# A decoder block on one core: the last 512 columns of the embedding gate, one token half after the other

## The chip, the cores and the metric

The kernel runs on one core of a Trainium2 chip. The metric is the device time of one execution in microseconds (us). TensorE (PE) does the matmuls, VectorE (DVE) and ScalarE (ACT) the elementwise work, GpSimd (POOL) a few small operations, and SyncE (SP) issues most transfers.

## The reference

One pre-norm decoder layer over 256 tokens and 2048 channels. Only the last step matters here:

```
x    = x + merged @ w_o                            # (256, 2048)
e    = rms_norm(p @ w_ple, g_ple_post)             # (256, 2048)
gate = sigmoid(rms_norm(x, g_ple) @ w_ple_gate)    # w_ple_gate is 2048 x 2048
x    = x + gate * e
out  = rms_norm(x, g_final)                        # over the 2048 channels of a token
```

The last norm needs the sum of squares over all 2048 channels of a token before any channel of that token can be written out. Inputs and outputs are fp32.

## The kernel before

Tokens are held in two halves of 128 (`h` is 0 or 1), one token per partition. Every large matrix product is made of three products, to keep fp32 precision: each weight and each activation is split into a high part (a copy in a reduced format, `fp32r`) and a low part (the rest), and high x high, high x low and low x high are added up in PSUM.

Weights stream in as *units*, `[128, 1024]` pieces of 512 KB. `issue_unit` issues the load of unit s + 7 on SyncE's queue into one of five `raw` buffers, `unit_hi` (L249, ScalarE) makes the high part of unit s + 3, `unit_lo` (L261, VectorE) the low part of unit s + 2; `hi` and `lo` have four buffers each. The loop over the units (`for s in range(NU)`) emits for each unit its matmuls, then these preparations, then what earlier units deferred. Tile's planner then sets the order on each engine by its own estimate of times and by what is ready; the order of the code is a priority and not the order of execution. A tile taken by `slot(tag, ...)` has one buffer for each tag, so a new tile waits until the last reader of the old one is done.

The embedding gate is four blocks of 512 output columns (`NC` = 4, `CW` = 512), each of eight units in `block_tm`. A unit holds 2 x 128 of the 2048 input channels (`kt`) for 512 columns. Here the activations `x2h` and `x2l` are the stationary operand (128 x 128) and the weights the moving one (128 x 512), so a unit has 12 matmuls, six for each token half, and the two halves fill two PSUM tiles side by side:

```
for h in range(2):
    for k in range(2):
        mm(ps, ah[:, kt, hs], hi[:, w], start=kt == 0, stop=False)
        mm(ps, ah[:, kt, hs], lo[:, w], start=False, stop=False)
        mm(ps, al[:, kt, hs], hi[:, w], start=False, stop=kt == kts - 1)
```

When a block is complete, `ev_pg` evacuates it for each half: the sigmoid with the token's scale (L638, ScalarE), times `e` (L641, VectorE), added to `x2` (L642), squared with the sum kept in `sq3` (L643, ScalarE), and times the gain of the last norm (L644, VectorE). `main_ps` has three PSUM tiles.

After the loop, once for both halves: `rstd_tok` reduces the sums (L625), scales them (L626) and takes the power -0.5 on GpSimd (L628); then `x2` is scaled in four pieces of 128 x 1024, one of each half on ScalarE (L1144) and one on VectorE (L1146), and each piece is written by a transfer of 512 KB on SyncE's queue (L1147). The tags `S2` and `S3` held `mh` and `ml`, the activations of the product with `w_o`, which is complete before the gate's blocks begin.

Of the kernel before, what the change touches and what calls it, by code (L numbers as in the profile page):

```python
# [10 lines left out]
F32R = mybir.dt.float32r  # L11
I32 = mybir.dt.int32
AF = mybir.ActivationFunctionType
ALU = mybir.AluOpType
AX = mybir.AxisListType
# [3 lines left out]
P = 128  # L19
T = 256  # L20
D = 2048
KT = 16
EPS = 1e-6
# [6 lines left out]
NC = 4  # L30
CW = 512
NWARM = 30
BUDGET = 1.3
TRLAG = 2

C_U, C_ZS, C_CQ, C_K, C_V, C_ZA, C_KI, C_GS, C_GA = 0, 1024, 2048, 2560, 2816, 3072, 4096, 4176, 6224

# [5 lines left out]
def block_kernel(ctx: ExitStack, tc: tile.TileContext, A: dict, out: bass.AP):  # L43
    nc = tc.nc
    V, S, G, PE = nc.vector, nc.scalar, nc.gpsimd, nc.tensor
    TT, STT = nc.vector.tensor_tensor, nc.vector.scalar_tensor_tensor

    cp = ctx.enter_context(tc.tile_pool(name="cp", bufs=1))
    wp = ctx.enter_context(tc.tile_pool(name="wp", bufs=4))
    ev = ctx.enter_context(tc.tile_pool(name="ev", bufs=2))  # L50
# [7 lines left out]
    def nm(s):  # L58
        uid[0] += 1
        return f"{s}_{uid[0]}"  # L60

    def slot(tag, shape, dt=F32):
        return cp.tile(shape, dt, tag=tag, name=nm(tag))

    def const(s, shape, dt=F32):
        return cp.tile(shape, dt, tag=s, name=s)
# [4 lines left out]
    def main_ps():  # L71
        return pm.tile([P, 512], F32, tag="main", name=nm("main"))
# [60 lines left out]
    mhalf = const("mhalf", [P, 2])  # L133
# [4 lines left out]
    def mm(o, l, r, start=True, stop=True, **kw):  # L138
        PE.matmul(o, l, r, start=start, stop=stop, **kw)  # L139
# [44 lines left out]
    units = []  # L184
    deferred = []
    step = [0]

    def defer(n, fn):
        deferred.append((step[0] + n, fn))

    def run_deferred(flush=False):
        while True:
            due = [d for d in deferred if flush or d[0] <= step[0]]
            if not due:
                return
            for d in due:
                deferred.remove(d)
            for d in due:
                d[1]()
# [36 lines left out]
            advance(t)  # L236

    his, los = {}, {}

    def unit_hi(u):  # L240
        if u >= len(units):
            return
        cols = units[u][2]
        hi = wp.tile([P, 1024], F32R, tag="hi", name=nm("hi"))
        src = raws[u][:, :cols]
        q = 2 if u < 3 else 1
        for i in range(q):
            o = slice(i * cols // q, (i + 1) * cols // q)
            S.copy(hi[:, o], src[:, o])  # L249
        his[u] = hi  # L250

    def unit_lo(u):
        if u >= len(units):
            return
        cols = units[u][2]
        lo = wp.tile([P, 1024], F32R, tag="lo", name=nm("lo"))
        src = raws.pop(u)
        q = 2 if u < 3 else 1
        for i in range(q):
            o = slice(i * cols // q, (i + 1) * cols // q)  # L260
            TT(lo[:, o], src[:, o], his[u][:, o].bitcast(F32), ALU.subtract)  # L261
        los[u] = lo
# [11 lines left out]
    def flush():  # L274
        run_deferred(True)
# [26 lines left out]
    def block_tm(act, kts, evac, needs=None):  # L302

        st = {}
        n = kts // 2

        def go(i, hi, lo):
            ah, al = act()
            if i == 0:
                st["ps"] = [main_ps(), None]  # L310
            for h in range(2):
                if st["ps"][h] is None:
                    st["ps"][h] = main_ps()
                ps = st["ps"][h]
                hs = slice(h * P, (h + 1) * P)
                for k in range(2):
                    kt = 2 * i + k
                    w = slice(k * CW, (k + 1) * CW)
# [3 lines that stand above are left out]
                if i == n - 1:  # L322
                    defer(h, lambda h=h, ps=ps: evac(h, ps))
        return [(lambda hi, lo, i=i: go(i, hi, lo), (needs or {}).get(i)) for i in range(n)]

    def add_tm(us):
        if len(us) == 1:
            us = us + [None]
        for a, b in zip(us[::2], us[1::2]):
            add_chunk(a, b)  # L330
# [10 lines left out]
        return (go, need)  # L341


    R = {}

    def hilo(ap):
        return ap[:, 0], ap[:, 1]
# [37 lines left out]
    u = slot("S5", [P, 8, T])  # L385
# [20 lines left out]
    for nb in range(8):  # L406
        add_chunk(*block_k16(xact, ev_u(nb), acc=first_acc(nb) if nb < 2 else None,
                             late=(6, 5, 3, 2)[nb] if nb < 4 else 1, split=nb < 2))
# [135 lines left out]
    def ccol(nb):  # L544
        return slice(nb * CW, (nb + 1) * CW)
# [11 lines left out]
    def tmp():  # L557
        R["ri"] += 1
        return R["ring"][:, R["ri"] % 4, :]
# [18 lines left out]
    def ev_ao(nb):  # L578
# [5 lines left out]
        def f(h, ps):  # L584
# [9 lines left out]
            if h == 1:  # L594
                defer(TRLAG, lambda: to_channels(R["os"], nb, tr))
        return f

    def ev_o(nb):
# [9 lines left out]
        def f(h, ps):  # L608
# [8 lines left out]
            if h == 1:  # L617
                defer(TRLAG, lambda: to_channels(R["x2"], nb, tr))
                if nb == NC - 1:
# [3 lines left out]
    def rstd_tok(sq, denom, tag):  # L623
        v = const(tag + "_v", [P, 2])
        V.tensor_reduce(v, sq, AX.X, ALU.add)  # L625
        V.tensor_scalar(v, v, 1.0 / denom, EPS, ALU.mult, ALU.add)  # L626
        c = const(tag + "_c", [P, 2])
        G.tensor_tensor(c, v, mhalf, ALU.pow)  # L628
        return c

    def ev_pg(nb):
        def f(h, ps):
            if nb == 0 and h == 0:
                R["sq3"] = const("sq3", [P, 2, NC])
            c = ccol(nb)
            x2 = R["x2"][:, h, c]
            s = tmp()
            S.activation(s, ps, AF.Sigmoid, scale=R["r2"][:, h:h + 1])  # L638

            def g():  # L640
                TT(s, s, R["e"][:, h, c], ALU.mult)  # L641
                TT(x2, x2, s, ALU.add)  # L642
                S.activation(s, x2, AF.Square, accum_out=R["sq3"][:, h, nb:nb + 1])  # L643
                TT(x2, x2, R["gfin"][:, c], ALU.mult)  # L644
            defer(0 if nb == NC - 1 else 1, g)
        return f


    sm = {}
# [444 lines left out]
        add_chunk(es[0][0], es[1][0])  # L1094
    for nb in range(NC):
        add_tm(block_tm(lambda: (R["mh"], R["ml"]), KT, ev_o(nb), {4: [pre_gate(A["xtok"], nb)]}))
    for nb in range(NC):
        add_tm(block_tm(lambda: (R["x2h"], R["x2l"]), KT, ev_pg(nb), {7: ["et"]} if nb == 0 else None))
    assert sum(1 for c in chunks if c[0] == "w") == NCH, (len(chunks), NCH)


# [18 lines left out]
    for s in range(NU):  # L1120
# [11 lines left out]
        unit_lo(s + 2)  # L1132
        issue_unit()
        pump(BUDGET)
    while deferred:
        step[0] += 1
        run_deferred()

    r3 = rstd_tok(R["sq3"], D, "r3")
    for h in range(2):  # L1140
        for q in range(2):
            o = R["x2"][:, h, q * 1024:(q + 1) * 1024]
            if q == 0:
                S.activation(o, o, AF.Copy, scale=r3[:, h:h + 1])  # L1144
            else:
                V.tensor_scalar(o, o, r3[:, h:h + 1], None, ALU.mult)  # L1146
            nc.sync.dma_start(out[h, :, q * 1024:(q + 1) * 1024], o)  # L1147


def _prepare(i):  # L1150
# [101 lines left out]
```

## Time and profile before

| what | value |
|---|---|
| runs shown, us | 809.04, 809.75, 854.57 (median 809.75) |
| profiled execution, us | 808.27 |
| its span, us | 806.5 |
| mean granted TensorE clock | 0.989 |
| TensorE busy | 783.9 us, 97% |
| VectorE, ScalarE busy | 575.3 us, 396.9 us |

The span goes from the first to the last instruction of the profiled execution; its own time is 1.77 us longer. A busy share is an average over the whole span. Start times in the rows below are us from the start of the span, and a granted clock of 1.00 is 2.4 GHz, 0.50 is 1.2 GHz.

### The profile page before, as it was taken

Reading aid. Unit: us, or ns where it says so; the run is one execution under the profiler, and the core shown is the slowest. Engines: PE = TensorE matmul, PEld = TensorE weight load, DVE = VectorE, ACT = ScalarE, POOL = GpSimd, SP = SyncE. Lnnn points to the kernel's source line nnn. Section 1 sums busy time; section 2 is a strip of 40 time slices with the busy share of each in tenths; the row PEclk is TensorE's granted clock in tenths of the full one; section 3 lists DMA queues with packets and bytes.
Section 4 is the critical chain, followed back from the end, with each engine's and each line's share of the span. In section 5 each row is a group of like instructions: output and inputs, shape, how many; then the busy total and the mean of one; then the engine's idle time right before and its main releaser. Section 6 shows DMA issues by size and latency. Waiting matters only on the chain.

```text
span 806.5 us, 12813 instructions
## 1 busy us (share of the span) xinstructions
PE 783.9 (97%) x5032; PEld 675.8 (84%) x5032; DVE 575.3 (71%) x891; ACT 396.9 (49%) x539; POOL 8.4 (1%) x17
## 2 busy tenths in 40 slices
PE   8999999999998999999999999999999999999993
PEld 7999987777997888899999987887887888888882
DVE  6999854999999954454668877756688555556662
ACT  7544545543444744453455474544445444445542
POOL 0000000000000000000000000000000000000000
PEclk9999999999999999999999999999999999999997
DMA  8868765346663676634754656666766665555522
GB/s 316 282 215 228 226 202 173 126 157 209 212 206 98 206 245 212 216 111 143 240 190 147 201 160 230 226 226 224 254 205 234 215 207 186 182 183 183 184 78 104
DMA packets 52060, 158.06 MB, mean 196 GB/s; under 512 B 5920, under 2 KB 12064, under 8 KB 51616
## 3 DMA queue, kind: packets, MB, share of 16 engines
q1 hardware_dynamic: 47104, 150.67, 56.6%
q10 hardware_dynamic: 4896, 6.58, 2.3%
q8 instruction: 39, 0.64, 0.3%
q14 instruction: 21, 0.17, 0.1%
HBM read 147.79 MB, written 8.39 MB: 194 GB/s over the span
## 4 chain that ended last, share of the span: by engine, by line
PE 38%; issue 11%; ACT 1%; DVE 0%; ACTq 0%; POOLq 0%; POOL 0%
PE main L139 34%; PE aux L139 2%; PE aux L147 1%; DVE lo L261 0%; ACT hi L249 0%; DVE S L1033 0%; ACT S L1144 0%; ACTq L1247 0%; ACT S L581 0%; POOLq L1247 0%; POOL r_c L628 0%; ACT S L1034 0%; PE small L147 0%; DVE r_v L626 0%; DVE r_v L625 0%
## 5 line engine op out<-in xcount | busy, mean ns | idle before, releaser
L261 DVE TENSOR_TENSOR lo<-raw,hi 128x1024 fp32r<-128x1024 f32 (+2 forms) x259 | 309.7, 1198 | 170.0 <-ACT hi L249 169.7
L249 ACT CAST hi<-raw 128x1024 fp32r<-128x1024 f32 (+2 forms) x259 | 265.4, 1031 | 319.7 <-PE main L139 282.7
L139 PE MATMUL main<-hi,S 128*128 128x512 f32 x544 | 175.2, 397 | 0.9 <-ACT S L1034 0.9
L139 PE MATMUL main<-lo,XH 128*128 128x512 f32 (+1 forms) x416 | 162.2, 390 | 1.9 <-DVE lo L261 1.9
L139 PE MATMUL main<-hi,XH 128*128 128x512 f32 (+1 forms) x416 | 163.4, 393 | 0.0
L139 PE MATMUL main<-hi,XL 128*128 128x512 f32 (+1 forms) x416 | 161.8, 389 | 0.0
L139 PE MATMUL main<-XH,hi 128*128 128x256 f32 x448 | 127.5, 285 | 1.8 <-ACT hi L249 1.8
L139 PE MATMUL main<-XH,lo 128*128 128x256 f32 x448 | 126.7, 283 | 1.9 <-DVE lo L261 1.9
L139 PE MATMUL main<-XL,hi 128*128 128x256 f32 x448 | 126.4, 282 | 0.0
L139 PEld LDWEIGHTS main<-hi,S 128*128 128x128 f32 x544 | 102.2, 188 | 25.3 <-ACT S L1034 1.6
L139 PE MATMUL main<-lo,S 128*128 128x512 f32 x272 | 107.8, 396 | 0.0
L139 PEld LDWEIGHTS main<-lo,XH 128*128 128x128 f32 x416 | 78.0, 188 | 20.4 <-DVE lo L261 3.5
L139 PEld LDWEIGHTS main<-hi,XH 128*128 128x128 f32 x416 | 78.0, 187 | 18.3
L139 PEld LDWEIGHTS main<-hi,XL 128*128 128x128 f32 x416 | 78.0, 187 | 17.4
L139 PEld LDWEIGHTS main<-XH,hi 128*128 128x128 f32 x448 | 85.1, 190 | 2.3 <-ACT hi L249 2.1
L139 PEld LDWEIGHTS main<-XH,lo 128*128 128x128 f32 x448 | 85.1, 190 | 2.1 <-DVE lo L261 2.1
L139 PEld LDWEIGHTS main<-XL,hi 128*128 128x128 f32 x448 | 85.1, 190 | 0.1
L139 PE MATMUL main<-S,hi 128*128 128x256 f32 x384 | 69.3, 283 | 0.1
L139 PEld LDWEIGHTS main<-lo,S 128*128 128x128 f32 x272 | 51.2, 188 | 11.0
L139 PEld LDWEIGHTS main<-S,hi 128*128 128x128 f32 x384 | 58.9, 188 | 1.7 <-issue 1.0
L139 PE MATMUL main<-S,lo 128*128 128x256 f32 x192 | 53.8, 280 | 0.0
L139 PEld LDWEIGHTS main<-S,lo 128*128 128x128 f32 x192 | 36.1, 188 | 0.0
(205 smaller groups left out, 616.5 us busy)
## 6 DMA issues: line engine op xcount, KB each, us to landing
raw<-in_wts_dram SPq DMA_DIRECT2D x247, 512.0 KB, 3.9
raw<-in_wvk_dram SPq DMA_DIRECT2D x8, 336.0 KB, 2.9
gs_d<-big ACTq DMA_DIRECT2D x8, 256.0 KB, 3.6
ga_d<-big ACTq DMA_DIRECT2D x8, 256.0 KB, 4.4
big<-gs_d SPq DMA_DIRECT2D x8, 256.0 KB, 4.6
big<-ga_d SPq DMA_DIRECT2D x8, 256.0 KB, 3.7
S<-in_grow_dram SPq DMA_DIRECT2D x2, 1024.0 KB, 6.0
big<-in_xtok_dram SPq DMA_DIRECT2D x8, 256.0 KB, 3.7
```

What stands on the lines that cost most here:

```text
L139: PE.matmul(o, l, r, start=start, stop=stop, **kw)
L147: PE.matmul(o, i, idn, is_transpose=True)
L249: S.copy(hi[:, o], src[:, o])
L261: TT(lo[:, o], src[:, o], his[u][:, o].bitcast(F32), ALU.subtract)
```

## The change

The first three blocks of the gate stay as they are. In the last block, the eight units in the loop serve the first token half alone (`last_half0`), with all 512 columns, six matmuls a unit; their high and low parts are kept. For this, four of the eight units take their parts from the tags `S2` and `S3` instead of the four turning buffers (`unit_tile`). After the loop the second token half is done in two parts of 256 columns, each over all eight units (96 matmuls with 256 columns instead of 48 with 512). Between the two parts `finish_half(0)` is written: sum of squares, power, scaling and output of the first half. The parts of the second half are evacuated one by one (`pg_part`), with a column of `sq3` for each, and `finish_half(1)` ends the kernel. The output is scaled and written in eight pieces of 128 x 512 (256 KB): those of the first half all on SyncE's queue, those of the second half alternately on ScalarE's and SyncE's.

```diff
--- before.py
+++ after.py
@@ -32,6 +32,7 @@
 NWARM = 30
 BUDGET = 1.3
 TRLAG = 2
+LASTU = 8
 
 C_U, C_ZS, C_CQ, C_K, C_V, C_ZA, C_KI, C_GS, C_GA = 0, 1024, 2048, 2560, 2816, 3072, 4096, 4176, 6224
 
@@ -236,12 +237,22 @@
             advance(t)
 
     his, los = {}, {}
+    R = {}
+
+    def unit_tile(tag, u):
+
+        j = u - (len(units) - LASTU)
+        if 0 <= j < LASTU - 4:
+            if j == 0:
+                R[tag + "x"] = slot("S2" if tag == "hi" else "S3", [P, LASTU - 4, 1024], F32R)
+            return R[tag + "x"][:, j, :]
+        return wp.tile([P, 1024], F32R, tag=tag, name=nm(tag))
 
     def unit_hi(u):
         if u >= len(units):
             return
         cols = units[u][2]
-        hi = wp.tile([P, 1024], F32R, tag="hi", name=nm("hi"))
+        hi = unit_tile("hi", u)
         src = raws[u][:, :cols]
         q = 2 if u < 3 else 1
         for i in range(q):
@@ -253,7 +264,7 @@
         if u >= len(units):
             return
         cols = units[u][2]
-        lo = wp.tile([P, 1024], F32R, tag="lo", name=nm("lo"))
+        lo = unit_tile("lo", u)
         src = raws.pop(u)
         q = 2 if u < 3 else 1
         for i in range(q):
@@ -341,7 +352,6 @@
         return (go, need)
 
 
-    R = {}
 
     def hilo(ap):
         return ap[:, 0], ap[:, 1]
@@ -628,22 +638,66 @@
         G.tensor_tensor(c, v, mhalf, ALU.pow)
         return c
 
+    def pg_part(ps, h, c, j, late=0):
+        x2 = R["x2"][:, h, c]
+        n = c.stop - c.start
+        s = tmp()[:, :n]
+        S.activation(s, ps[:, :n], AF.Sigmoid, scale=R["r2"][:, h:h + 1])
+
+        def g():
+            TT(s, s, R["e"][:, h, c], ALU.mult)
+            TT(x2, x2, s, ALU.add)
+            S.activation(s, x2, AF.Square, accum_out=R["sq3"][:, h, j:j + 1])
+            TT(x2, x2, R["gfin"][:, c], ALU.mult)
+        defer(late, g)
+
     def ev_pg(nb):
         def f(h, ps):
             if nb == 0 and h == 0:
-                R["sq3"] = const("sq3", [P, 2, NC])
-            c = ccol(nb)
-            x2 = R["x2"][:, h, c]
-            s = tmp()
-            S.activation(s, ps, AF.Sigmoid, scale=R["r2"][:, h:h + 1])
-
-            def g():
-                TT(s, s, R["e"][:, h, c], ALU.mult)
-                TT(x2, x2, s, ALU.add)
-                S.activation(s, x2, AF.Square, accum_out=R["sq3"][:, h, nb:nb + 1])
-                TT(x2, x2, R["gfin"][:, c], ALU.mult)
-            defer(0 if nb == NC - 1 else 1, g)
+                R["sq3"] = const("sq3", [P, 2, NC + 1])
+                V.memset(R["sq3"], 0.0)
+            pg_part(ps, h, ccol(nb), nb, 0 if nb == NC - 1 else 1)
         return f
+
+    last = []
+
+    def last_half0():
+
+        ev = ev_pg(NC - 1)
+
+        def go(i, hi, lo):
+            last.append((hi, lo))
+            if i == 0:
+                R["ps0"] = main_ps()
+            last_mm(R["ps0"], 0, i, slice(0, CW))
+            if i == LASTU - 1:
+                defer(0, lambda: ev(0, R["ps0"]))
+        return [(lambda hi, lo, i=i: go(i, hi, lo), None) for i in range(LASTU)]
+
+    def last_mm(ps, h, i, c):
+        hi, lo = last[i]
+        ah, al = R["x2h"], R["x2l"]
+        n = c.stop - c.start
+        hs = slice(h * P, (h + 1) * P)
+        for k in range(2):
+            kt = 2 * i + k
+            w = slice(k * CW + c.start, k * CW + c.stop)
+            mm(ps[:, :n], ah[:, kt, hs], hi[:, w], start=kt == 0, stop=False)
+            mm(ps[:, :n], ah[:, kt, hs], lo[:, w], start=False, stop=False)
+            mm(ps[:, :n], al[:, kt, hs], hi[:, w], start=False, stop=kt == KT - 1)
+
+    def finish_half(h):
+        v = const(f"r3v{h}", [P, 2])
+        V.tensor_reduce(v[:, 0:1], R["sq3"][:, h], AX.X, ALU.add)
+        V.tensor_scalar(v[:, 0:1], v[:, 0:1], 1.0 / D, EPS, ALU.mult, ALU.add)
+        G.tensor_tensor(v[:, 1:2], v[:, 0:1], mhalf[:, 0:1], ALU.pow)
+        for q in range(4):
+            o = R["x2"][:, h, ccol(q)]
+            if q % 2 == 0:
+                S.activation(o, o, AF.Copy, scale=v[:, 1:2])
+            else:
+                V.tensor_scalar(o, o, v[:, 1:2], None, ALU.mult)
+            (nc.scalar if h and q % 2 == 0 else nc.sync).dma_start(out[h, :, ccol(q)], o)
 
 
     sm = {}
@@ -1094,8 +1148,9 @@
         add_chunk(es[0][0], es[1][0])
     for nb in range(NC):
         add_tm(block_tm(lambda: (R["mh"], R["ml"]), KT, ev_o(nb), {4: [pre_gate(A["xtok"], nb)]}))
-    for nb in range(NC):
+    for nb in range(NC - 1):
         add_tm(block_tm(lambda: (R["x2h"], R["x2l"]), KT, ev_pg(nb), {7: ["et"]} if nb == 0 else None))
+    add_tm(last_half0())
     assert sum(1 for c in chunks if c[0] == "w") == NCH, (len(chunks), NCH)
 
 
@@ -1132,19 +1187,20 @@
         unit_lo(s + 2)
         issue_unit()
         pump(BUDGET)
-    while deferred:
-        step[0] += 1
-        run_deferred()
-
-    r3 = rstd_tok(R["sq3"], D, "r3")
-    for h in range(2):
-        for q in range(2):
-            o = R["x2"][:, h, q * 1024:(q + 1) * 1024]
-            if q == 0:
-                S.activation(o, o, AF.Copy, scale=r3[:, h:h + 1])
-            else:
-                V.tensor_scalar(o, o, r3[:, h:h + 1], None, ALU.mult)
-            nc.sync.dma_start(out[h, :, q * 1024:(q + 1) * 1024], o)
+    flush()
+    parts = [slice(0, CW // 2), slice(CW // 2, CW)]
+    pss = []
+    for j, c in enumerate(parts):
+        pss.append(main_ps())
+        for i in range(LASTU):
+            last_mm(pss[j], 1, i, c)
+        if j == 0:
+            finish_half(0)
+    base = (NC - 1) * CW
+    for j, c in enumerate(parts):
+        pg_part(pss[j], 1, slice(base + c.start, base + c.stop), NC - 1 + j)
+        flush()
+    finish_half(1)
 
 
 def _prepare(i):
```

## Rows read from the trace of the kernel before

**Rows 1.** The page's first part: busy us of each engine (share of the span).

```profile
PE 783.9 (97%) x5032; PEld 675.8 (84%) x5032; DVE 575.3 (71%) x891; ACT 396.9 (49%) x539; POOL 8.4 (1%) x17
```

**Rows 2.** Windows: us, PE, PEld, DVE, ACT, POOL busy, PEclk, DMA share, GB/s.

```profile
770.95:773.75 2.80, 2.80 (x13) 2.25 (x13) 2.52 (x4) 2.25 (x4) 0.00 (x0) 1.00 0.58 190
```

**Rows 3.** Timeline of the tail: start us, us, engine, line, operation [idle].

```profile
792.96 0.39 PE L139 MATMUL main<-hi,XL 128*128 128x512 f32 x1
...
793.38 0.69 ACT L638 ACTIVATE S<-main,r_c 128x512 f32<-128x512 f32 x1 [0.71 <-PE main L139]
...
794.83 0.69 DVE L642 TENSOR_TENSOR S<-S,S 128x512 f32<-128x512 f32 x1
...
795.55 0.63 ACT L643 ACTIVATE S<-S 128x512 f32<-128x512 f32 x1 [0.67 <-DVE S L642]
...
796.92 0.15 DVE L625 TENSOR_REDUCE r_v<-sq 128x2 f32<-128x8 f32 x1
...
797.36 0.69 POOL L628 TENSOR_TENSOR r_c<-r_v,mhalf 128x2 f32<-128x2 f32 x1 [90.98 <-DVE r_v L626]
...
798.08 1.42 DVE L1146 TENSOR_SCALAR S<-S,r_c 128x1024 f32<-128x1024 f32 x2 [0.80 <-POOL r_c L628]
798.86 2.94 SPq L1147 DMA_DIRECT2D out_dram<-S  x4
```

**Rows 4.** Short windows of the output and of an earlier load, columns as above.

```profile
799.50:800.00 0.50, 0.00 (x0) 0.00 (x0) 0.00 (x0) 0.50 (x1) 0.00 (x0) 0.50 0.63 254
...
802.00:802.50 0.50, 0.00 (x0) 0.00 (x0) 0.00 (x0) 0.00 (x0) 0.00 (x0) 0.50 1.04 410
...
804.50:805.00 0.50, 0.00 (x0) 0.00 (x0) 0.00 (x0) 0.00 (x0) 0.00 (x0) 0.50 0.73 279
...
555.20:556.00 0.80, 0.80 (x6) 0.62 (x5) 0.66 (x3) 0.45 (x2) 0.00 (x0) 1.00 0.79 264
```

**Rows 5.** Timeline of TensorE, starts of matmuls of 512 and of 256 columns.

```profile
354.74 0.28 PE L139 MATMUL main<-XL,hi 128*128 128x256 f32 x1
...
361.37 0.28 PE L139 MATMUL main<-XH,hi 128*128 128x256 f32 x1
...
779.89 0.39 PE L139 MATMUL main<-hi,XH 128*128 128x512 f32 x1
```

**Rows 6.** Timeline of SyncE, VectorE and ScalarE ahead of the last units.

```profile
745.32 25.53 SPq L97 DMA_DIRECT2D raw<-in_wts_dram  x10
...
772.07 1.22 DVE L261 TENSOR_TENSOR lo<-raw,hi 128x1024 fp32r<-128x1024 f32 x1 [0.24 <-ACT hi L249]
...
773.81 0.68 DVE L644 TENSOR_TENSOR S<-S,S 128x512 f32<-128x512 f32 x1
...
782.23 1.05 ACT L249 CAST hi<-raw 128x1024 fp32r<-128x1024 f32 x1 [1.75 <-PE main L139]
...
783.31 1.23 DVE L261 TENSOR_TENSOR lo<-raw,hi 128x1024 fp32r<-128x1024 f32 x1 [1.57 <-ACT hi L249]
```

**Rows 7.** DMA issues: tensors, queue, count, KB each, median us to landing.

```profile
raw<-in_wts_dram SPq DMA_DIRECT2D x247, 512.0 KB, 3.9
...
S<-in_pT_dram SPq DMA_DIRECT2D x1, 256.0 KB, 2.7
```

**Rows 8.** Groups by line and form, 256 columns: busy us, mean ns of one.

```profile
L418 ACT ACTIVATE big<-t 128x256 f32<-128x256 f32 x16 | 6.7, 420 | 34.0 <-DVE t L416 34.0
...
L416 DVE TENSOR_TENSOR t<-main,row 128x256 f32<-128x256 f32 x16 | 6.6, 414 | 0.6 <-PE main L139 0.6
...
L982 DVE TENSOR_SCALAR S<-S,sums 128x256 f32<-128x256 f32 x8 | 2.4, 347 | 0.0
```

**Rows 9.** One line's instructions: transfer issues on ScalarE, ns min/median/max.

```profile
L426 ACTq DMA_DIRECT2D gs_d<-big x8: 326/326/327, 133.9 to 211.9; - x8
```

**Rows 10.** Windows early in the kernel, columns as in rows 2.

```profile
7.00:10.00 3.00, 2.26 (x6) 1.12 (x6) 2.85 (x7) 3.00 (x8) 0.00 (x0) 1.00 1.00 386
...
12.00:14.00 2.00, 2.00 (x12) 2.00 (x11) 0.62 (x2) 2.00 (x4) 0.00 (x0) 0.50 1.03 420
```

## The prediction

> **What bounds the kernel now.** I read the page first: TensorE works 97% of the span [rows 1], so what happens beside it is worth nothing until TensorE stops, and a change at the end of the program is worth what it does to the last stretch. Of the last block of columns one row shows the pattern: in its first 2.80 us TensorE is full, VectorE is busy 2.52 us [rows 2]. A block is eight units of 2.80 us, so the last one runs from 770.95 to 793.35.
>
> The timeline of the tail comes next [rows 3]. The last matmul ends at 793.35 (792.96 + 0.39) and the span at 806.5: 13.15 us without a matmul, 1.6% of the span. To be seen there is one chain: sigmoid of the second token half at 793.38, multiply and add (the add at 794.83), square 795.55, reduce 796.92, after a scalar step the power on GpSimd 797.36, scaling by ScalarE and VectorE 798.08, first output transfer issued 798.86. That is 4.73 us from the last matmul to the scaling, and 0.78 from there to the issue.
>
> Then the narrow windows [rows 4]: data begin in the window 799.50 to 800.00 at 254 GB/s, which at a full rate near 405 is 0.31 us of it, so at 799.69, 0.83 after the issue. The windows between are full, as the one at 802.00 (410). The last has 279 GB/s, so the data end at 804.84. All 2.10 MB leave in 5.15 us behind the last token's scale, and 1.66 us remain to the end of the span. So the tail is a chain of small operations (5.5), a start (0.8), a transfer at full rate (5.15) and a fixed end (1.7).
>
> **The change part by part.** *TensorE.* The first token half keeps 48 matmuls of 512 columns; the second gets 96 of 256 instead of 48 of 512. The 512-column starts at 779.89 and 792.96 are 56 starts apart, 0.2333 us each [rows 3, 5]. The 256-column starts at 354.74 and 361.37 are also 56 apart, 0.1184 [rows 5]. 96 x 0.1184 is 11.37 against 48 x 0.2333 = 11.20: +0.17 us. In those earlier rows the 256 columns are activations and here weights; the bounds are half of 0.2333 (nothing lost) and 0.2333 (nothing gained by half the width, +11.2 us); I take 0.1184, same shape, same type, with a weight load for each. Last matmul then ends at 793.52.
>
> *Supply of the split weights.* Each unit's pieces serve only six matmuls in the loop, so TensorE wants a unit every 1.40 us, not 2.80. Before, the last high part starts at 782.23, released by TensorE, since four buffers turn, and the last low part at 783.31 [rows 6]. With four of the last eight units in two other slots (whose last readers, the output projection, ended with the block before these four), the last unit takes the buffer that the ninth-last gives back at 770.95 instead of 782.15: it may start 11.2 us earlier and is wanted 9.8 us earlier (780.75 instead of 790.55). So its slack grows by 1.4. The raw loads take 3.9 us to land and are five deep [rows 7]; ten units in the 20 us ahead are 5.2 MB or 260 GB/s, under the 410 of [rows 4]. VectorE has 1.23 for each low part and six times 0.69 for the evacuation of the block before: 10 x 1.23 + 4.1 = 16.4 us in the 25 us before 780.75. Cost nothing, with that slack as cover. Without it the price is in the rivals. The order on an engine isn't the written one: the low part at 772.07 stands ahead of the final multiply at 773.81 [rows 6], which is written before it, so a planner fills the waits and I don't expect a low part stuck behind an evacuation.
>
> *First token half.* Its sigmoid can start at about 782.2. The chain as before, 4.73 us, then scaling, puts its four output transfers near 787 to 788; 1.05 MB at 405 GB/s is 2.6 us, done by about 792. This stands under the 11.4 us of the second half's matmuls and costs nothing, and so do one more reduce, scalar step, power (GpSimd has nothing else then) and four transfer issues on SyncE, behind which no load is queued any more: the ten last raw loads are issued by 770.87 [rows 6]. If the cover failed, 2.58 us of transfer would come back to the end. The first part of the second half is complete at 787.9 and its evacuation (about 2.5 us of chain) ends before 793.5 too. Setting the sums to zero is one small operation three blocks earlier: nothing.
>
> *The chain at the end.* It now works on 256 columns. An activation of 256 columns takes 0.42 [rows 8] where the square of 512 takes 0.63 [rows 3], so the sigmoid's 0.69 becomes an estimated 0.46, and with 0.03 before and behind it the multiply starts at 794.04; multiply and add take 0.41 + 0.03 each [rows 8]: square at 794.92. From square to reduce it was 1.37 at 512 [rows 3]; the two 512-column operations in it become shorter by about 0.21 and 0.28 (0.63 and 0.69 against 0.42 and 0.41): 0.88, reduce at 795.80. The 0.44 from there to the power and the 0.72 to the scaling don't depend on the width: scaling at 796.96, 3.44 after the last matmul instead of 4.73: -1.29.
>
> *Scaling and issue.* The pieces are now 512 wide, two on each engine. VectorE took 1.42 for two of 1024 and takes 0.35 for one of 256 [rows 3, 8]; for 512 an estimate midway, 0.48. First issue at 797.47, 0.51 after the scaling began instead of 0.78: -0.27. On ScalarE a transfer issue of 0.33 [rows 9] may stand between its two scalings; its second piece is then issued at about 798.7, and three pieces of 0.65 us keep the data flowing till about 800.25, so it isn't waited for.
>
> *Output.* Half the bytes are left: 2.58 instead of 5.15 us: -2.58. No row shows 256 KB stores on two queues with nothing else. The near end is the rate of [rows 4]; the far end below nothing would be a faster rate, which the full windows exclude. The other bound is the single 256 KB load, which took 2.7 us from issue to landing [rows 7]: in that stretch the loads moved at 264 GB/s [rows 4], which would make 1.05 MB 3.97 us, 1.4 worse. I take the rate of [rows 4], as the nearer row: same direction, same source, nothing beside it.
>
> Here a rule speaks against the change. Four transfers of 512 KB followed one another and kept the full rate [rows 4], so between them no pause shows. The Trainium skill, page DMA: Bandwidth & Descriptors, section Bandwidth, says to batch transfers to 1 MiB or more for 75% of the peak; its fit (section Anatomy of one DMA) has about 2 us of fixed cost in each, so four of 256 KB one by one would be an estimated 10.4 us and eat the whole gain. By the trace the fixed part overlaps when several are queued. What a lone mechanism of this sort would do is a rival below.
>
> The sum: +0.17 - 1.29 - 0.27 - 2.58 = -3.97. The span goes from 806.5 to 802.5, the profiled execution from 808.27 to 804.3. The runs shown are 809.04 and 809.75 (median 809.75, with one at 854.57), 0.8 to 1.5 above the profiled one; from their middle, 809.4, the forecast is 805.4.
>
> **The rivals.** (a) The output moves at 264 GB/s: +1.4, so 806.8. For: rows of half the length, two queues. Against: the full windows.
> (b) The splits come late. If the last low part ended where it does now, 784.54 (783.31 + 1.23), TensorE would start its last unit's low half there instead of at 780.98: +3.56, so 809.0, no change left. For: VectorE is nearly full at the block's border [rows 2]. Against: the buffers above. If TensorE then has gaps, the clock may go: early in the kernel, after 3 us in which TensorE was busy for 2.26, it stood at half, 1.2 GHz, from 12 to 14 us at least [rows 10], 2 us that cost 1.0 of matmul time; 810.0.
> (c) The planner places the first half's finish late, so that all 2.1 MB still leave at the end: +2.58, so 808.0. Against: that finish is written ahead of the second part's matmuls and waits for nothing of them. This is the case in which the change doesn't do what it says.
> (d) Slower than before: transfers of one queue or of two wait for each other's landing. Four times 2.7 from 797.47 end at 808.3, and with some 1.1 to the end the span is 809.4, 2.9 over the present: 812.3. It decides once the four take 6.5 us instead of 2.58. Against it the full windows at 410 GB/s speak directly [rows 4]. The rule of the Trainium skill, page DMA: Bandwidth & Descriptors, section Bandwidth, would bring it about.
> (e) A bit more gain, the chain being shorter than my widths say: 804.4.
>
> **How the numbers follow.** Forecast 0.63, (a) 0.13, (b) 0.09, (c) 0.06, (d) 0.02, (e) 0.07. The range 803.9 to 808.4 holds the forecast with the scatter of the runs (0.7), (a), (c) and (e), some 0.89 less what a median may stray; (b) and (d) are left out. 2% is 16 us, about what a measurement of this kernel tells from no change. The tail itself is only 13.15 us, so no case here is faster by more: 0.01 for that. Slower by 16 us needs a stall or a clock that no case has, such as the 0.2333 bound with late splits: 0.02. Within 2%: 0.97.
>
> **What would show it.** Right: TensorE without a gap from 771 to about 793.5 at full clock; last matmul to scaling about 3.5 us; output in two lots, 1.05 MB ending before 793 and 1.05 MB from about 798.3 to 800.9; span near 802.5. Wrong: gaps of TensorE behind low parts in the last eight units; 256-column starts over 0.12 us apart; a second lot below 350 GB/s; first-half scaling after 793.

## The result and the profile after

The changed kernel takes 798.99 us (median of 4 runs, 798.54 to 799.33) against 809.39 for the kernel before beside it: a ratio of 0.988, 95% interval [0.9869, 0.9892]. One of the four runs of the kernel before was a slow one, 854.57 us, and the ratio leaves it out. The gain is within 2%, but far outside the scatter, and the time lies below the predicted range of 803.9 to 808.4. The profiled execution took 799.28 us with a span of 797.3, so the span fell by 9.2 us where 4.0 were forecast.

The page's first part, TensorE's row of the kernel after, answers to [rows 1]:

```profile
PE 776.6 (97%) x5080; PEld 674.5 (85%) x5080; DVE 576.2 (72%) x899; ACT 397.6 (50%) x544; POOL 8.8 (1%) x18
```

TensorE is busy 7.3 us less than in [rows 1], although the change gives it 48 matmuls more. To see where, I cut the end of the kernel after near the last block's start, near the end of its first half and at its last matmul. Windows view (us, then busy time of PE, PEld, DVE, ACT and POOL, PEclk, DMA share, GB/s), as in [rows 2]:

```profile
766.00:776.95 10.95, 10.95 (x50) 8.99 (x49) 4.96 (x8) 2.96 (x6) 0.00 (x0) 1.00 0.00 0
776.95:788.22 11.27, 11.20 (x96) 11.00 (x95) 4.45 (x10) 3.62 (x8) 0.55 (x1) 1.00 0.26 95
788.22:797.30 9.08, 0.00 (x0) 0.00 (x0) 2.38 (x7) 2.32 (x5) 0.55 (x1) 0.63 0.31 116
```

TensorE has no gap up to 788.15, with the clock granted in full. Where the block starts is seen in the timeline of TensorE (start, us, instruction), at its first matmul behind the last one of the block before. Kernel before:

```profile
770.55 0.39 PE L139 MATMUL main<-hi,XL 128*128 128x512 f32 x1
770.79 0.40 PE L139 MATMUL main<-hi,XH 128*128 128x512 f32 x1
```

and kernel after, where the high parts of this block's first units lie in a slot (`S`):

```profile
765.55 0.39 PE L140 MATMUL main<-hi,XL 128*128 128x512 f32 x1
765.78 0.62 PE L140 MATMUL main<-S,XH 128*128 128x512 f32 x2
```

**The block starts 5.01 us earlier: that much was gained before it, in blocks that the change doesn't touch.** From there its matmuls take 22.37 us (to 788.15) where they took 22.56 (770.79 to 793.35 [rows 3]), and the tail behind them 9.15 instead of 13.15. So the 9.2 us are 5.01 ahead of the changed stretch, 0.19 in its matmuls and 4.00 in its tail. The tail, as a timeline of the kernel after, answers to [rows 3]:

```profile
787.87 0.28 PE L140 MATMUL main<-hi,XL 128*128 128x256 f32 x1
788.25 0.47 ACT L645 ACTIVATE S<-main,r_c 128x256 f32<-128x256 f32 x1 [3.57 <-PE main L140]
...
789.67 0.42 ACT L650 ACTIVATE S<-S 128x256 f32<-128x256 f32 x1 [0.95 <-DVE S L649]
...
790.55 0.15 DVE L691 TENSOR_REDUCE r3v<-sq 128x1 f32<-128x5 f32 x1
...
791.56 0.88 DVE L699 TENSOR_SCALAR S<-S,r3v 128x512 f32<-128x512 f32 x2 [0.67 <-POOL r3v L693]
792.07 0.81 SPq L700 DMA_DIRECT2D out_dram<-S  x2
```

The chain is the one of [rows 3] with narrower operations: 788.15 (787.87 + 0.28) to the scaling at 791.56 is 3.41 us, and the first issue follows 0.51 later. The half-microsecond windows of the kernel after, one of the first output lot and those of the second, answer to [rows 4]:

```profile
785.50:786.00 0.50, 0.50 (x7) 0.50 (x6) 0.00 (x0) 0.00 (x0) 0.00 (x0) 1.00 0.34 115
...
792.50:793.00 0.50, 0.00 (x0) 0.00 (x0) 0.00 (x0) 0.39 (x1) 0.00 (x0) 0.50 0.16 53
793.00:793.50 0.50, 0.00 (x0) 0.00 (x0) 0.00 (x0) 0.00 (x0) 0.00 (x0) 0.50 1.01 385
793.50:794.00 0.50, 0.00 (x0) 0.00 (x0) 0.00 (x0) 0.00 (x0) 0.00 (x0) 0.50 1.02 389
794.00:794.50 0.50, 0.00 (x0) 0.00 (x0) 0.00 (x0) 0.00 (x0) 0.00 (x0) 0.50 1.01 361
...
795.50:796.00 0.50, 0.00 (x0) 0.00 (x0) 0.00 (x0) 0.00 (x0) 0.00 (x0) 0.50 0.38 135
```

The first lot thins out from the window at 785.50, while TensorE works. The second fills 0.07 of the window at 792.50 (53 of about 385) and 0.18 of the last (135 of 385): from 792.93 to 795.68, 2.75 us for 1.05 MB, so 381 GB/s.

Now the part that wasn't touched. Starts of 256-column matmuls in the timeline of the kernel before, in a stretch that both kernels spend on the same products:

```profile
49.77 0.28 PE L139 MATMUL main<-XH,hi 128*128 128x256 f32 x1
...
59.95 0.28 PE L139 MATMUL main<-XH,lo 128*128 128x256 f32 x1
```

and in that of the kernel after:

```profile
49.74 0.28 PE L140 MATMUL main<-XH,hi 128*128 128x256 f32 x1
...
59.94 0.28 PE L140 MATMUL main<-XH,hi 128*128 128x256 f32 x1
```

In 10.2 us the kernel before starts 86 of them, 0.1184 us apart, the kernel after 90, 0.1133 apart: same form, same clock. Windows of 20 us with 256 columns and of 60 us with 512, kernel before:

```profile
45.00:65.00 20.00, 20.00 (x171) 20.00 (x170) 19.75 (x28) 8.71 (x9) 0.00 (x0) 1.00 0.55 184
270.00:330.00 60.00, 60.00 (x259) 48.18 (x258) 35.18 (x32) 29.15 (x32) 0.00 (x0) 1.00 0.69 229
```

and kernel after:

```profile
45.00:65.00 20.00, 20.00 (x179) 20.00 (x178) 19.74 (x29) 9.40 (x9) 0.00 (x0) 1.00 0.55 184
270.00:330.00 60.00, 60.00 (x264) 49.24 (x263) 33.96 (x31) 28.55 (x30) 0.00 (x0) 1.00 0.71 228
```

TensorE is busy throughout in both and the clock is 1.00; only the count differs, 171 to 179 and 259 to 264. The engine isn't waited for less: each matmul holds it for less time.

The instructions ahead of the last block stand in the same order on every engine in the two programs, except for one more `memset` of `sq3`. What differs is addresses in SBUF, read from the two programs as built. `sq3` grew from `[P, 2, 4]` to `[P, 2, 5]`, 32 to 40 bytes a partition, which the allocator rounds to 64; every tile behind it moved by 32 bytes, `raw`, `hi` and `lo` among them (`hi` from 173888 to 173920), while the activations (`XH` at 35104, the slots `S2` to `S7`) stayed. **Theory:** the pace of matmuls depends on where their two operands lie against each other. **Rivals:** the `memset` shifts the planner's order or timing; the second queue or the changed end acts on the start in some way; the absolute address of the weights counts, not the difference.

### The profile page after: what moved, and what is told of

Its sections match the earlier page's. It is cut to its first block, busy times and chain, and to the rows that moved or that the text cites. A ratio compares the mean times of both kernels' runs of the same rounds, so it can differ in the third digit from the quotient of the medians.

```text
span 797.3 us, 12926 instructions
## 1 busy us (share of the span) xinstructions
PE 776.6 (97%) x5080; PEld 674.5 (85%) x5080; DVE 576.2 (72%) x899; ACT 397.6 (50%) x544; POOL 8.8 (1%) x18
## 4 chain that ended last, share of the span: by engine, by line
PE 47%; issue 1%; DVE 1%; ACT 1%; DMA 1%; POOLq 0%; POOL 0%; DVEq 0%; ACTq 0%
PE main L140 44%; PE aux L140 2%; PE aux L148 1%; DMA zld<-za_d 1%; ACT S L697 0%; DVE lo L272 0%; DVE S L1087 0%; ACT hi L260 0%; ACT S L591 0%; DVE t L1045 0%; ACT S L650 0%; DVE S L649 0%; DVE S L648 0%; ACT S L645 0%; DVE S L651 0%
## 5 line engine op out<-in xcount | busy, mean ns | idle before, releaser
L272 DVE TENSOR_TENSOR lo<-raw,hi 128x1024 fp32r<-128x1024 f32 (+2 forms) x255 | 304.8, 1197 | 156.3 <-ACT hi L260 156.1
L260 ACT CAST hi<-raw 128x1024 fp32r<-128x1024 f32 (+2 forms) x255 | 261.4, 1031 | 302.9 <-PE main L140 268.3
L140 PE MATMUL main<-lo,XH 128*128 128x512 f32 (+2 forms) x408 | 155.9, 382 | 2.4 <-DVE lo L272 2.4
L140 PE MATMUL main<-hi,XH 128*128 128x512 f32 (+2 forms) x408 | 156.9, 385 | 0.0
L140 PE MATMUL main<-hi,XL 128*128 128x512 f32 (+2 forms) x408 | 156.0, 382 | 0.0
```

## The experiments

Each kernel ran beside the kernel before on its chip, which took 808.36 us beside e1 to e4, 808.19 beside e5 to e8, 808.45 beside f1 to f4 and 808.5 beside g1 and g2. All times are medians of runs, in us; a ratio is to the kernel before.

**e1: the old kernel, addresses moved.** The tile is wider, and only the old columns are used.

```diff
-                R["sq3"] = const("sq3", [P, 2, NC])
+                R["sq3"] = const("sq3", [P, 2, NC + 1])
-    r3 = rstd_tok(R["sq3"], D, "r3")
+    r3 = rstd_tok(R["sq3"][:, :, :NC], D, "r3")
```

> The kernel before, with one thing altered: the tile of the last norm's sums is declared with five columns instead of four (40 bytes a partition instead of 32, the fifth unused), so that everything behind it in SBUF, raw, hi and lo among it, lies 32 bytes further on; the order on every engine is the same. Theory A (the 5 us gained ahead of the changed stretch come from where the weight parts lie): 4 to 6 us faster than before, about 804.5, with 256-column starts 0.1133 instead of 0.1184 us apart between 40 and 67 us and 512-column starts 0.229 instead of 0.2333 between 270 and 330 us. Theory B (they come from the zeroing of the sums at the start or from the order of the program): no change, 809. Theory C (scatter between executions): no change within 1 us.

Measured: 802.29, ratio 0.9923 [0.9909, 0.9938], span 800.6. Nothing of the change is in this kernel, and 6.1 us are gone. Its windows show the pace of the kernel after:

```profile
45.00:65.00 20.00, 20.00 (x179) 20.00 (x178) 19.80 (x29) 9.41 (x9) 0.00 (x0) 1.00 0.59 197
270.00:330.00 60.00, 60.00 (x264) 49.23 (x263) 33.27 (x30) 28.10 (x29) 0.00 (x0) 1.00 0.67 226
```

**e2: the changed kernel, addresses put back.** The two tiles of the last scale share one, which takes the 32 bytes out again.

```diff
-        v = const(f"r3v{h}", [P, 2])
+        if h == 0:
+            R["r3v"] = const("r3v", [P, 2, 2])
+        v = R["r3v"][:, h]
```

> The changed kernel with the two small tiles of the last norm joined in one, so that raw, hi and lo lie at the addresses of the kernel before; order on the engines unchanged. Theory A: the gain ahead of the last block goes, the gain of the tail stays: about 804 (the forecast 805.4 less the 0.3 us by which the tail did better), 256-column starts back at 0.1184. Theories B and C: 799 as the changed kernel.

Measured: 804.33, ratio 0.9948 [0.9931, 0.9965], span 802.5; the changed end is worth 4.03 us, and 3.97 had been forecast. The old counts are back:

```profile
45.00:65.00 20.00, 20.00 (x171) 20.00 (x170) 19.59 (x29) 8.94 (x9) 0.00 (x0) 1.00 0.53 181
270.00:330.00 60.00, 60.00 (x259) 48.17 (x258) 34.95 (x32) 28.98 (x32) 0.00 (x0) 1.00 0.67 227
```

The tail in its timeline (last matmul, scaling, first issue):

```profile
793.04 0.27 PE L140 MATMUL main<-hi,XL 128*128 128x256 f32 x1
...
796.72 0.88 DVE L701 TENSOR_SCALAR S<-S,r3v 128x512 f32<-128x512 f32 x2 [0.67 <-POOL r3v L695]
797.24 0.81 SPq L702 DMA_DIRECT2D out_dram<-S  x2
```

The last matmul ends at 793.31, 0.04 before that of [rows 3], the scaling is 3.41 behind it and the issue 0.52 behind that. So e1 and e2 split the result in two parts that nearly add up to it: 5.9 us of span from the addresses (806.5 to 800.6) and 4.0 from the change itself (to 802.5), 9.9 together, where the kernel after has 9.2.

**e3: the old kernel with the `memset`.**

```diff
                 R["sq3"] = const("sq3", [P, 2, NC])
+                V.memset(R["sq3"], 0.0)
```

> The kernel before with the zeroing of the sums alone, addresses unchanged. Theory A: 809.4 as before, within 1 us. Theory B: 804 to 805.

Measured: 808.7, ratio 1.0005 [0.9996, 1.0015]. The extra instruction does nothing; that rival is out.

**e4: the changed kernel, all output on SyncE's queue.**

```diff
-            (nc.scalar if h and q % 2 == 0 else nc.sync).dma_start(out[h, :, ccol(q)], o)
+            nc.sync.dma_start(out[h, :, ccol(q)], o)
```

> The changed kernel with all eight output transfers on the queue of SyncE. My step that the second queue brings no bandwidth: 799.0, within 0.5 us. A rival in which the second queue is worth what its earlier issue saves: up to 1 us slower, 800.

Measured: 798.31, ratio 0.9874 [0.9859, 0.9888], span 796.0. The second queue brings nothing: the ratio with one queue isn't above that with two. The time is 0.69 below the 799.0 that was expected within 0.5; the two intervals overlap.

**e5 to e7: how far, and which operand.** e5 moves `hi` and `lo` of the old kernel by 64 bytes instead of 32 (and uses the old columns alone, as e1 does). e6 puts 32 bytes ahead of `XH`, so that activations and weights both move. e7 does the same and takes 32 bytes out behind the activations, so that only the activations move.

```diff
# e5
-                R["sq3"] = const("sq3", [P, 2, NC])
+                R["sq3"] = const("sq3", [P, 2, 3 * NC])
# e6 and e7
-    first = const("first", [P, 2])
+    first = const("first", [P, 10])[:, 0:2]
# e7 besides
-        v = const(tag + "_v", [P, 2])
+        vc = const(tag + "_vc", [P, 2, 2]) if tag == "r3" else None
+        v = const(tag + "_v", [P, 2]) if vc is None else vc[:, 0]
-        c = const(tag + "_c", [P, 2])
+        c = const(tag + "_c", [P, 2]) if vc is None else vc[:, 1]
```

> The kernel before with raw, hi and lo 64 bytes further on (the sums' tile declared with 12 columns), order of the program unchanged. In the kernel before hi and lo lie at a multiple of 64 and the activations XH and XL at 32 beyond one; in the changed kernel all lie at 32 beyond one. If only the place within 64 bytes counts: no gain, 808.4, 256-column starts 0.1184 between 40 and 67 us. Rival, any other place is better than the old one or the period is 128 bytes or more: 802 to 806.

> The kernel before with 32 bytes put ahead of XH, so that activations, weights and all else behind lie 32 bytes further on: XH, XL and the large slots at a multiple of 64, hi and lo at 32 beyond one. Theory R (what counts is that both operands of a matmul lie alike within 64 bytes): they still differ by 32, no gain, 808. Theory H (the place of the weight parts alone counts): fast as with the 32 bytes behind XH, about 802.3, 0.1133 between 40 and 67 us.

> The same 32 bytes ahead of XH, and 32 bytes taken out behind the slots, so that hi and lo lie where they did and the activations alone are moved: all at a multiple of 64. Theory R: fast, about 802.3. Theory H: slow, 808.4, 0.1184 between 40 and 67 us.

Measured: e5 809.04, ratio 1.0009 [0.9999, 1.0018] (its 256-column starts are 0.1173 apart, not the 0.1184 expected); e6 808.25, ratio 0.9997 [0.9988, 1.0007]; e7 801.58, ratio 0.9915 [0.99, 0.993]. e6 has `hi` where e1 has it, at 173920, and none of e1's gain; its windows are those of the kernel before:

```profile
45.00:65.00 20.00, 20.00 (x171) 20.00 (x170) 20.00 (x29) 8.83 (x9) 0.00 (x0) 1.00 0.58 198
270.00:330.00 60.00, 60.00 (x259) 48.17 (x257) 35.16 (x32) 29.18 (x32) 0.00 (x0) 1.00 0.68 229
```

So the absolute address of the weights isn't it. e7 has `hi` where the kernel before has it and gains 6.6 us, the time of theory R; but it gains in another way than e1, in the matmuls of 512 columns and not in those of 256:

```profile
45.00:65.00 20.00, 20.00 (x169) 20.00 (x168) 19.79 (x29) 8.44 (x9) 0.00 (x0) 1.00 0.58 195
270.00:330.00 60.00, 60.00 (x266) 49.71 (x265) 35.60 (x33) 30.54 (x33) 0.00 (x0) 1.00 0.69 233
```

What the paces follow is the address of `hi` less that of `XH`, modulo 256 (`hi` and `lo` have the same remainder): 32 in the kernel before, e2, e3 and e6, 64 in the kernel after, e1 and e4, 96 in e5, 0 in e7. At this point 256 is a guess; f1 to f3 test it.

**e8: the changed kernel, second half in one part of 512 columns.**

```diff
-    parts = [slice(0, CW // 2), slice(CW // 2, CW)]
+    parts = [slice(0, CW)]
```

> The changed kernel with the second token half done in one part of 512 columns (48 matmuls) instead of two of 256. By my terms the chain at the end gets longer by 1.29 and TensorE's work shorter by 0.17: 1.1 us slower than the changed kernel, about 800 where that has 799. Rival, the two parts give nothing since another work ends last: the same as the changed kernel.

Measured: 800.24, ratio 0.9895 [0.9881, 0.991], span 798.5, so 1.2 above the kernel after. The two intervals overlap, so the sizes rest on the traces. The block's first matmul and the tail in its timeline:

```profile
765.93 0.62 PE L140 MATMUL main<-S,XH 128*128 128x512 f32 x2
...
787.73 0.39 PE L140 MATMUL main<-hi,XL 128*128 128x512 f32 x1
...
792.70 0.88 DVE L699 TENSOR_SCALAR S<-S,r3v 128x512 f32<-128x512 f32 x2 [0.67 <-POOL r3v L693]
```

The scaling is 4.58 behind the last matmul instead of 3.41: the two parts are worth the narrow chain, 1.17 us. The last matmul ends at 788.12, as in the kernel after (788.15), but the block began 0.15 later than there, at 765.93. So it takes 22.19 us instead of 22.37: the two parts cost TensorE 0.18.

**f1 to f3: the difference of the kernel after set to 128, 192 and 0.** All output on one queue, and the sums' tile wider by 64, 128 and 192 bytes (8, 16, 24 columns in two rows).

```diff
-                R["sq3"] = const("sq3", [P, 2, NC + 1])
+                R["sq3"] = const("sq3", [P, 2, NC + 1 + 8])[:, :, :NC + 1]
```

> The changed kernel with all output on one queue and raw, hi and lo moved on by 64 bytes more, so that hi lies 128 beyond XH when both are taken modulo 256 (the kernel before 32, the changed kernel 64, the kernel with the activations alone moved 0). Starts of 256 and of 512 columns so far: 32 apart 0.1184 and 0.2333, 96 apart 0.1173 and 0.2333, 64 apart 0.1133 and 0.2289, 0 apart 0.1200 and 0.2267. If the period is 128 bytes: as 0 apart, about 797.2. If 256: another pair, between 795 and 803.

> The same moved by 128 bytes, hi 192 beyond XH modulo 256. If the period is 128 bytes: as the changed kernel on one queue, 798.3, with 0.1133 and 0.2289. If 256: another pair, 795 to 803; below 797 it would be the best place so far.

> The same moved by 192 bytes, hi and XH alike modulo 256, the activations left where they are. If only the difference between the two counts: 0.1200 and 0.2267 as where the activations alone were moved, and the two gains add up, 808.2 - 6.6 - 4.0 = 797.6, with one queue perhaps 797.2. If the absolute place counts too: 798 to 804.

Measured: f1 804.22, ratio 0.9946 [0.9931, 0.9961]; f2 803.46, ratio 0.9936 [0.9921, 0.9951]; f3 797.98, ratio 0.9872 [0.9857, 0.9887]. At 128 and 192 what remains is the gain of e2, the change alone, or up to 1 us more. Both times lie above the 795 to 803 that was expected. At 0 all is there, by 192 bytes of unused space. The windows with 512 columns of f1, f2 and f3, in this order:

```profile
270.00:330.00 60.00, 60.00 (x260) 48.65 (x259) 35.48 (x32) 29.48 (x32) 0.00 (x0) 1.00 0.69 229
270.00:330.00 60.00, 60.00 (x259) 48.35 (x258) 34.38 (x31) 29.06 (x32) 0.00 (x0) 1.00 0.67 225
270.00:330.00 60.00, 59.87 (x264) 49.58 (x265) 36.78 (x35) 30.84 (x33) 0.00 (x0) 1.00 0.67 232
```

f1 and f2 differ from e7 and e1 by 128 bytes and have other counts (266 and 264 there), so the period isn't 128, nor 64: theory R, alike within 64 bytes, would have made f1 and f2 fast. f3 and e7 lie 256 bytes apart when the difference is taken modulo 512, with `XH` at other addresses too, and have the same starts, 0.1200 and 0.2267: the period is 256, and in the stretches with `XH` and `XL` the difference counts and not the addresses themselves.

**f4: the first half's finish moved to the end** (addresses of `hi` and `XH` as in the kernel after). One reduce and one power serve both halves.

```diff
-        if j == 0:
-            finish_half(0)
...
-    finish_half(1)
+    r3 = rstd_tok(R["sq3"], D, "r3")
+    finish_half(0, r3)
+    finish_half(1, r3)
```

> The changed kernel with the scaling and the output of the first token half held back to the end, as one reduce, power and scaling for both halves; matmuls, parts and addresses as in the changed kernel. By my sum the half of the output that was hidden comes back: 2.6 us slower than the changed kernel, and up to 0.5 more for eight scalings instead of four, so 801.6 to 802.1 where that has 799.0. Rival, the output's end is not what ends last: 799.

Measured: 801.85, ratio 0.9915 [0.9899, 0.9932], span 800.5; 2.8 above the kernel after by the ratios (0.0035 of 808.45), the forecast's 2.58 for half of the output and a little more.

**g1 and g2: addresses chosen on purpose.** The slots `S2` to `S7` hold the activations of other stages and have differences of their own. g1 keeps 64 to `XH` and brings those of `S6` and `S7` to 64 (`S3` stays at 128); g2 sets `S3` to 0 besides. Both write all output on one queue. The core of g2:

```diff
-        f = const("fre", [P, 2, 32])
+        f = const("fre", [P, 2, 48])[:, :, :32]
-        ct = slot("S3", [P, 2, 2, 32, 32])
+        ct = slot("S3", [P, 4096 + 48])[:, :4096].rearrange("p (a b t c) -> p a b t c", a=2, b=2, t=32)
```

with small tiles joined to win the space back; g1 has `4096 + 16`, leaves `fre` and widens `sq3` by 24 columns.

> The changed kernel with all output on one queue, XH, XL, hi and lo where it has them (64 apart modulo 256), and the slots S7 and S6 moved so that their operands (the normed query latents, the gated state outputs, the attention outputs) are 64 instead of 128 from hi as well. If a matmul's pace follows from the difference of its own two operands modulo 256, by the pairs seen so far: the stage near 442 us of the kernel before goes from 0.1187 to 0.1133 or 0.1178, the attention product from 0.2324 to 0.2289; 576 x 0.0009 to 0.0054 and 192 x 0.0035 make 1.2 to 3.8 us, so 794.5 to 797.1 against 798.3. If something else that moved along was the cause: no gain, 798.3.

> The same, and S3 moved so that its operands (state outputs before their projection, the low part of the merged activations) are 0 instead of 128 from hi, where 512-column starts were 0.2267 instead of 0.2324: 192 and 128 such matmuls, 1.8 us, and up to 1 us more where high and low parts alternate; 792 to 795.5, the fastest so far. If the pairs don't add up like this: as the kernel with S7 and S6 moved alone.

Measured: g1 795.75, ratio 0.9844 [0.9828, 0.9861]; g2 793.9, ratio 0.9818 [0.9803, 0.9833], span 791.2, the fastest of all here. The window that holds most of the product with `w_o`, whose low activations lie in `S3`, in g1:

```profile
620.00:700.00 80.00, 80.00 (x359) 65.14 (x358) 43.64 (x51) 38.77 (x56) 0.70 (x1) 1.00 0.56 195
```

and in g2:

```profile
620.00:700.00 80.00, 80.00 (x364) 65.88 (x363) 44.74 (x51) 38.77 (x56) 0.69 (x1) 1.00 0.57 199
```

359 to 364 matmuls in 80 us, by the place of `S3`. Both times are within what was expected. But pairs don't simply add up in every product: in e7 the activations of this one, `S2` and `S3`, lie 0 and 64 from the weights, the two fast rows of the table at the end, and its count is that of the kernel before, where they lie at 32 and 96. The kernel before, then e7:

```profile
620.00:700.00 80.00, 80.00 (x360) 65.13 (x359) 45.01 (x50) 37.19 (x52) 0.00 (x0) 1.00 0.59 199
620.00:700.00 80.00, 80.00 (x360) 65.38 (x359) 43.80 (x49) 37.90 (x53) 0.00 (x0) 1.00 0.57 200
```

## Why the prediction was wrong

**What failed** is a step that the prediction took at its start: "a change at the end of the program is worth what it does to the last stretch." So the sum, +0.17 - 1.29 - 0.27 - 2.58 = -3.97, counts the changed stretch alone and sets the 771 us ahead of it at no change. They became 5.01 shorter, because `hi` and `lo` moved by 32 bytes against the activations and the matmuls of the stages before changed their pace: e1, with the 32 bytes alone, gains 6.1 us, and e2, with the change alone, 4.0. The diff had shown it, in the line that gives `sq3` one more column: a tile changes size, so addresses change. Among the five rivals none was for a change that acts where it isn't written. The range was built from the same cases and left it out with them. The signs by which the prediction wanted to be judged lay in the last stretch too, and but for coming 5 us earlier they came out as for a right forecast.

**The terms themselves**, each by its own measure:

- *TensorE*, +0.17 forecast: for what it stands for, two narrow parts instead of a wide one, it was right, since e8 undoes them and the block takes 0.18 less. All the same the block took 0.19 less than before at the new addresses, and with `hi` and `lo` back, in e2, the last matmul ends 0.21 ahead of the forecast 793.52. There the term left out that the change itself puts half of the block's weights into `S2` and `S3`, 0 and 192 bytes from the activations modulo 256. TensorE's timeline of e2 at the block's start, at the first unit from the turning buffers and at the second half:

```profile
770.76 0.62 PE L140 MATMUL main<-S,XH 128*128 128x512 f32 x2
...
776.26 0.39 PE L140 MATMUL main<-hi,XH 128*128 128x512 f32 x1
...
781.86 0.41 PE L140 MATMUL main<-S,XH 128*128 128x256 f32 x2
```

  The first 24 matmuls take 5.50 us, the next 24 take 5.60, which is 0.10 of the 0.21. The 95 steps from 781.86 to 793.04 take 0.1177 each where the forecast took 0.1184, another 0.07.
- *The chain at the end*, -1.29: 3.41 from the last matmul to the scaling, forecast 3.44. Right; e8 undoes it and pays 1.17 on the path.
- *Scaling and issue*, -0.27: 0.51, as forecast.
- *Output*, -2.58: 2.75 us instead of the forecast 2.58 for the half that is left. The rate was 381 GB/s, not 405, a term mis-sized by 0.17. The measure of the hidden half is f4: 2.8 us when it isn't hidden. That e2 meets the forecast span of 802.5 so closely is in part luck: its last matmul is 0.21 earlier than forecast, and the 9.19 us behind it are 0.21 longer than the forecast 8.98.
- *Supply* and *first half*, at nothing: the windows of the last block show TensorE full up to 788.15. By the timeline of the kernel after, VectorE's last low part starts at 768.61 and ends at 769.83, 5.9 us ahead of the forecast's need (780.75 less the 5.01 of the earlier start); the first half is scaled at 781.52 and issued from 782.03:

```profile
768.61 1.22 DVE L272 TENSOR_TENSOR lo<-raw,hi 128x1024 fp32r<-128x1024 f32 x1
...
781.52 0.88 DVE L699 TENSOR_SCALAR S<-S,r3v 128x512 f32<-128x512 f32 x2 [0.66 <-POOL r3v L693]
...
782.03 10.85 SPq L700 DMA_DIRECT2D out_dram<-S  x6
```

So rivals (b) and (c) are out by the trace. (a), the rate of the early load, is out by the full windows of the second lot; (d), transfers one by one, too: four transfers of 256 KB filled them, at 361 to 389 GB/s in those shown, so the 10.4 us that the prediction worked out from the Trainium skill (page DMA: Bandwidth & Descriptors, section Anatomy of one DMA, a fit for transfers issued from GpSimd) isn't paid here. The 804.33 of e2 is also the time of (e), 804.4, but not for its reason: the chain was as long as forecast, and the kernel before took 808.36 beside e2 where the forecast started from 809.4.

**Why addresses gave less than they could.** The pace gains 4.3% in the first of the windows above and 1.9% in the second, but some of TensorE's waits grew. The two largest kinds in the kernel before (us in total, times, longest):

```profile
PE main L139 <- DVE lo L261: 3.8, 5, 1.9
PE main L139 <- ACT hi L249: 1.8, 1, 1.8
```

and in the kernel after:

```profile
PE main L140 <- DVE lo L272: 4.3, 5, 1.9
PE main L140 <- ACT hi L260: 2.7, 1, 2.7
```

That is 1.4 us more waiting. That TensorE came earlier than the parts it needed would explain it, but no run isolates that. Stages with their activations in the slots became slower besides: near 442 us, where they lie in `S7`, the matmuls of the kernel before start 0.1173 apart and those of the kernel after 0.1187, since that difference went from 96 to 128. g1, which sets it to 64, has 0.1133 there.

**What stays open.** Why the remainder of the address counts isn't shown by any run; a conflict of the two operands' reads would fit, no more. Nor is it settled what decides in some stretches at a difference of 64 between 0.1133 and 0.1178: near 215 us the kernel after and e1 have 0.1178, e4 0.1133, though the kernel after and e4 have the same addresses and the same order of matmuls. So in such stretches the difference alone doesn't settle the pace.

## What to carry to other kernels

Before a diff is costed, ask what it does to the addresses of tiles that it doesn't name: one more column in a tile of a few bytes moved 5 us here, more than the change itself brought. When a kernel differs from its forecast, count the matmuls in an equal window of a stretch that both have in common; equal busy time with another count is a pace, not a wait, and needs no story about the change. And where TensorE sets the time, try the placement of its operands by itself: moving tiles by a few unused bytes (g2) gave 4.4 us beyond e4, on top of a change that was meant to give 4.

## What the runs showed of the hardware

Start to start of matmuls with a weight load each, at a granted clock of 1.00 (2.4 GHz), by the address of the weights' split parts less that of the activations, modulo 256, from the starts in the traces:

| difference, bytes | 256 columns, us | 512 columns, us | kernels |
|---|---|---|---|
| 0 | 0.1200 | 0.2267 | e7, f3 |
| 32 | 0.1184 | 0.2333 | before, e2, e3, e6 |
| 64 | 0.1133 (in places 0.1178) | 0.2289 | after, e1, e4 |
| 96 | 0.1173 | 0.2333 | e5 |
| 128 | 0.1187 | 0.2324 | f1 |
| 192 | 0.1178 | 0.2333 | f2 |

In the rows of 256 columns the weights are the operand that is loaded and the activations move; in those of 512 it is the other way round, so the two columns differ in that as well as in width. No row is best in both: 64 for 256 columns, 0 for 512. Differences of 160 and 224 weren't run against `XH`. The Trainium skill, page TensorE: Matmul & The Clock Gate, section Step-by-step: what each phase is for, says that loading the next tile's weights takes no read bandwidth from the running matmul, the two having ports of their own. No run here shows which reads take how long, so none tests this directly. But with the same matmuls in the same order (e1 and e7) the pace moved by up to 6%, 0.1133 to 0.1200, with the place of one operand against the other, which that section doesn't mention.

Transfers of 256 KB, with rows of 2 KB, left at 381 GB/s over the second lot of the kernel after (361 to 397 in its full windows), a little under the 407 of the 512 KB pieces (2.10 MB in 5.15 us), and one queue (e4) did as well as two.
